# Raw first products of each later layer, its input in two VectorE operations and one ScalarE operation a tile, and the third output gate's product ahead of the first head

## The chip, the cores and the metric

The kernel runs on one core of one Trainium2 chip. The metric is the device time of one execution in microseconds; below it is the median of three runs. Smaller is better.

## The reference

A first block (gated feed-forward, attention with a state-space mixer, a second feed-forward, a gated embedding) is followed by two layers of the same form, each of which joins a gated linear recurrence and a matrix memory with heads. Sequence length is 512, model width 1024, all in float32. What the change touches is the end of the first block and the beginning of each later layer, cut to this:

```python
gate = jax.nn.sigmoid(rmsnorm(h, norm_ple[i]) @ w_ple_gate[i])
h = h + gate * (p[i] @ w_ple[i])
x = rmsnorm(h, norm_final)                      # end of the first block
for l in range(DEPTH_2):                        # the two later layers
    mod = c_act @ w_ada[l] + b_ada[l]
    shift, scale, gate = jnp.split(mod, 3, axis=-1)
    h = rms_norm(x, norm_g[l]) * (1.0 + scale[:, None, :]) + shift[:, None, :]
    u = h @ w_in[l]                             # 1024 x 5120
    rg_x, rg_z, ml_x, ml_o, ml_z = jnp.split(u, split_pts, axis=-1)
    y_rg = rglru(conv(rg_x), ...) * jax.nn.silu(rg_z)
    y_ml = mlstm_branch(ml_x, ml_o, ...) * jax.nn.silu(ml_z)
    y = jnp.concatenate([y_rg, y_ml], axis=-1) @ w_out[l]
    x = x + gate[:, None, :] * y
```

A norm is a factor for each position; so `h @ w_in` is the factor times the product of the unnormalised x (with the gain in it), plus `shift @ w_in`, which is the same for all positions.

## The kernel before

Activations lie transposed: model width in 8 tiles of 128 partitions, 512 positions along the free axis. A weight block is 128x128. Each float32 product is made of three matmuls in the engine's rounded float32 form (`mm3`, lines 125 to 127): high weight by high input, high weight by low input, low weight by high input. So each input tile is split in two (`xnh`, `xnl`), and so are the weights: the stream brings them in chunks of 8 blocks (512 KB), ScalarE makes the high half of a chunk (`whi`, line 96) and VectorE the low half (`wlo`, line 98). A chunk is split when the fifth block of the chunk two before it is fetched (`Stream.get`), unless `hold` is set; the split stands in the queues of both engines at that place of the program.

Each engine works through its own list in order. A norm is made in steps: ScalarE squares each tile (`nsq`, `nacc`, line 149), VectorE and GpSimd add them up, TensorE sums over the partitions by matmuls with ones (line 165, `early` for the first seven tiles, `mean` for the last), VectorE takes the root in ten short operations (`ncol`), TensorE transposes it to a row (line 195), and ScalarE copies the row (`nrow`, line 198).

The stages that matter here, in order:

- `ffn2`, the second feed-forward. A list of small pieces of work for the later layers (`second_prepare`: the products of `w_ada`, and the load and split of `p`) is dealt out between its products.
- `ple`, the gate stage: for each of 8 output tiles m a product of 8 blocks, a second product of 2 blocks for tile m-1, and then on VectorE the multiplication with the row (line 1282), on ScalarE tanh (1283), and on VectorE two operations that give the new `h[m]` (1287, 1288). `on_tile` squares it for two norms: the closing norm of the first block, and that of the first layer (`between` combines both).
- the first seam (`between`) and the second (`renorm`, ahead of layer 1): norm, then `modulate`, which makes the 8 input tiles from h, row, gain and shift: multiply by the row (`mt`, alternately on VectorE and GpSimd, line 1330), the affine on VectorE (`mx`, 1338) and with the high half on ScalarE (1337), and the low half on VectorE (1341).
- `layer`: first four products, `w_in` tiles 16 to 19, side by side (`proj4`), with VectorE's convolutions behind them (`ml_in`); then the order that `LAYER` writes out by hand. P*m* is the product of tile m, U*m* its use; 0 to 7 feed the recurrence, 24 to 27 are the output gates. `qkv` are the products of the first head pairs, `rg` the recurrence's gates, `hn` a head. `aside`, a list that `pump` works off twice a product, holds the residual's own norm and its store in layer 0.
- `out`: eight products of 16 blocks; each adds to the residual that is read back from memory (`xr`).

The order around the change, before: `P24 U24 P25 U25 P20 qkv0 ...` and further on `rg0 rq0 vr0 P26 U26 hn0 rs0 ...`.

Of the kernel before, what the change touches and what calls it, by code (L numbers as in the profile page):

```python
# [31 lines left out]
T = 512  # L32
DM = 1024
# [5 lines left out]
R1, R2 = 0.27, 0.26  # L39
# [8 lines left out]
GAPS = {"base": 288, "ffn1": 320, "ffn2": 0, "lay": 320, "mix2": 224, "ple": 256}  # L48
# [81 lines left out]
class Norm:  # L130
# [3 lines left out]
    def __init__(self, k, n, pool=None, tail=False):  # L134
        self.k, self.n, self.i = k, n, 0
        self.tail, self.head = tail, None
        self.pool = pool or k.work
        self.acc = []

    def add(self, src, scale=1.0):  # L140


        k, i = self.k, self.i
        own = i < 2 or (self.tail and i == self.n - 1)
        if own:
            sq = self.pool.tile([128, T], F32, name="nacc", bufs=3 if self.pool is k.work else 6)
# [3 lines left out]
        if own:  # L150
            self.acc.append(sq)
        elif i % 2:
            k.nc.gpsimd.tensor_add(self.acc[1], self.acc[1], sq)  # L153
        else:
            k.nc.vector.tensor_add(self.acc[0], self.acc[0], sq)
        self.i += 1
        if self.i == self.n - self.tail:
            eng = k.nc.vector if self.tail else k.nc.gpsimd
            eng.tensor_add(self.acc[0], self.acc[0], self.acc[1])
# [1016 lines left out]
def second_prepare(k, pool, ins):  # L1176
# [15 lines left out]
    for l in range(2):  # L1192
# [83 lines left out]
def ple(k, pool, xs, norm, pt, on_tile, early):  # L1276
# [3 lines left out]
    def gate1(m, pg):  # L1280
        ts[m] = pool.tile([128, T], F32, name="pleg", bufs=2)
# [16 lines left out]
    for m in range(8):  # L1298
# [12 lines left out]
        k.ws.hold = m == 7  # L1311
# [4 lines left out]
    early()  # L1316


def modulate(k, l, norm, gg, scr):
# [3 lines left out]
    xs, ts = [], []  # L1323
    with k.tc.tile_pool(name=f"modulate{l}", bufs=3) as tmp:
        def scale(d):
            t = tmp.tile([128, T], F32, name="mt", bufs=4)
            if d % 2:
                nc.gpsimd.tensor_mul(t, k.h[d], norm.row)
            else:
                v.tensor_mul(t, k.h[d], norm.wide)  # L1330
            ts.append(t)
        for d in range(3):
            scale(d)
        for d in range(8):
            x = tmp.tile([128, T], F32, name="mx")
            hi, lo = xtile(k, "xnh"), xtile(k, "xnl")
            nc.scalar.activation(hi, ts[d], AF.Identity, scale=gg[:, d:d + 1], bias=L.mod[:, d:d + 1])
            v.tensor_scalar(x, ts[d], gg[:, d:d + 1], L.mod[:, d:d + 1], op0=OP.mult, op1=OP.add)
            if d + 3 < 8:
                scale(d + 3)  # L1340
            v.tensor_sub(lo, x, hi.bitcast(F32))
            xs.append((hi, lo))
            if d == 1:
                k.ws.release()
            k.dbg(f"hh{l}{d}", x)
    return xs


def between(k, scr, nf, ng):

    nc, v = k.nc, k.nc.vector
    gg = k.work.tile([128, 8], F32, name="gg")
    gf = k.vec[:, VEC["norm_final"][0]:VEC["norm_final"][0] + 8]
    v.tensor_mul(gg, gf, k.lay[0].gs)
    nf.part1(root=False)
    ng.mean()
    ms = k.work.tile([128, 4], F32, name="nmt", bufs=2)
    v.scalar_tensor_tensor(ms, nf.ms, 1e-6, ng.ms, op0=OP.mult, op1=OP.add)  # L1360
    ng.col = k.work.tile([128, 4], F32, name="ncol", bufs=2)
    rsqrt(k, ng.col, ms)
    ng.part2()
    xs = modulate(k, 0, ng, gg, scr)
    rsqrt(k, nf.col, nf.ms)

    def root():
        nf.part2()

    def residual(d):  # L1370
        v.scalar_tensor_tensor(k.h[d], k.h[d], gf[:, d:d + 1], nf.row, op0=OP.mult, op1=OP.mult)
        nc.sync.dma_start(scr["x"][d], k.h[d])
        k.dbg(f"x2{d}", k.h[d])
    return xs, [root] + [lambda d=d: residual(d) for d in range(8)]


def renorm(k, l, norm, scr):
    norm.part1()
    norm.part2()
    xs = modulate(k, l, norm, k.lay[l].gs, scr)  # L1380
    return xs, [lambda d=d: k.nc.sync.dma_start(scr["x"][d], k.h[d]) for d in range(8)]


LAYER = """P24 U24 P25 U25 P20 qkv0 D P21 U20 U21 mi2 vw P22 U22 P23 U23 qkv1 D mi3 vw P0 U0 qkv2 vw D qkv3 g0 vw g1 P1 U1 ri0 P8 g2 D P9 U8 g3 hw0 hs0 U9 rg0 rq0 vr0 P26 U26 hn0 rs0 rs1 rz0 rz1 vr1 P27 U27 hw1 f0 P2 U2 hs1 D P3 U3 ri1 u F0 P32 U32 P33 U33 D rg1 rq1 hn1 rs2 P10 U10 P11 f1 rs3 U11 P29 U29 rz2 hw2 P28 rz3 vr2 U28 P4 U4 hs2 P5 U5 ri2 u P34 rg2 rq2 F1 U34 P35 U35 hn2 rs4 P12 D P13 f2 D U13 U12 rs5 P31 rz4 vr3 hw3 P30 rz5 U30 U31 P6 U6 P7 U7 ri3 D u hs3 D P36 F2 rg3 U36 P37 rq3 hn3 rs6 P14 U37 rs7 u P15 f3 U14 U15 rz6 P38 D F3 rz7 U38 D P39 U39 vw"""
# [82 lines left out]
def layer(k, l, xs, aside, ins, scr, norm, out):  # L1467
# [4 lines left out]
    with ExitStack() as st:  # L1472
        pool = st.enter_context(k.tc.tile_pool(name=f"lay{l}", bufs=1))
        room(pool, "lay")
# [51 lines left out]
        G = k.ps.tile([128, T], F32, name="pm", bufs=2)  # L1526
# [393 lines left out]
        def x_read(m):  # L1920
            if m < 8:
                xr[m] = xtile(k, "xr", F32)
                nc.sync.dma_start(xr[m], scr["x"][m])
        k.phase = f"out{l}"
        for m in range(8):
            x_read(m)
        for m in range(8):
            if l and m == 7:
# [10 lines left out]
            norm.add(k.h[m])  # L1939
VEC = {}  # L1940
# [20 lines left out]
def body(tc, ins, out, dbg):  # L1961
    nc = tc.nc
    with ExitStack() as ctx:
# [16 lines left out]
               "y": dp.tile([512, 512], F32, name="scr_y"), "x": dp.tile([8, 128, T], F32, name="scr_x"),  # L1980
# [70 lines left out]
        k.const2 = pool("const2")  # L2051
        k.onehot = k.const2.tile([8, 4, 128], F32R, name="onehot")
# [4 lines left out]
        with tc.tile_pool(name="prep2", bufs=1) as pp:  # L2057
# [4 lines left out]
            pt = []  # L2062
            ple_p = tc.tile_pool(name="ple", bufs=1)
            with ple_p as lp:
                room(lp, "ple")
                def load_p():
                    for d in range(2):
                        t = lp.tile([128, T], F32, name=f"p{d}")
                        nc.sync.dma_start(t, ins["pT"][d * 128:(d + 1) * 128])
                        pt.append(t)  # L2070

                def split_p():
                    for d in range(2):
                        pt[d] = split_plain(k, lp, pt[d], f"pp{d}", 1)
                k.fill.steps += [(0.1, load_p), (0.1, lambda: None), (1.2, split_p)]
                swiglu(k, st["xs"], st["norm"], "ffn2_w1", "ffn2_w3", "ffn2_w2", (6, 6, 5, 5),
                       lambda d: feed("norm_ple", d), R2, ((0, 1, 5), (1, 0, 7)), "ffn2")
                k.fill.drain()
                k.phase = "ple"
                with tc.tile_pool(name="sums", bufs=1) as np_:  # L2080
                    nf, ng = Norm(k, 8, np_, True), Norm(k, 8, np_, True)

                    def done(m):
                        nf.add(k.h[m])
                        ng.add(k.h[m], k.v("norm_final", m))
                    ple(k, lp, st["xs"], st["norm"], pt, done, lambda: (nf.early(), ng.early(0.0)))
                    xs, aside = between(k, scr, nf, ng)
        norm = None
        for l in range(2):
            norm = Norm(k, 8, tail=True)  # L2090
            k.phase = f"layer{l}"
            layer(k, l, xs, aside, ins, scr, norm, out)
# [132 lines left out]
```

## Time and profile before

| | |
|---|---|
| time, median of 3 runs | 1997.68 us (1996.73 to 1998.62) |
| the profiled execution | 1996.86 us, its span 1995.1 us |
| TensorE matmul busy | 1931.2 us, 97% |
| VectorE busy | 1311.4 us, 66% |
| ScalarE busy | 821.4 us, 41% |
| GpSimd busy | 164.4 us, 8% |
| mean granted TensorE clock | 0.982 of full speed |

The profile is of one execution. A busy time counts the instructions of an engine, not what waits; a row of a timeline gives the start of a group of like instructions in us from the start of the span, its length, and in brackets the idle time ahead of it with the engine that ended it. The time of the stages can be read from the names: the gate stage is 1061 to 1118 us, the first seam begins there, and the second at 1554.

### The profile page before, as it was taken

How to read it: one execution, taken by the hardware profiler on the slowest of the kernel's cores; microseconds unless marked ns; L12 is line 12 of the kernel's file. 1: busy time of each engine (PE TensorE's matmuls, PEld its weight loads, DVE VectorE, ACT ScalarE, POOL GpSimd, SP SyncE). 2: the span in 40 equal slices, each digit the busy share in tenths (PEclk: the TensorE clock that was granted, in tenths of full speed). 3: DMA queues.
4: the chain of work that ended last, by engine and by line, in shares of the span. 5: the costliest groups of instructions: out<-in, count | busy, mean ns of one | idle time of the engine just before them, and what ended most of it. 6: DMA issues, size and time to landing. Idle time of an engine off the chain costs nothing. (4 is left out here: it accounts for less than half of the span.)

```text
span 1995.1 us, 24709 instructions
## 1 busy us (share of the span) xinstructions
PE 1931.2 (97%) x9320; PEld 1581.3 (79%) x9320; DVE 1311.4 (66%) x2157; ACT 821.4 (41%) x1233; POOL 164.4 (8%) x225
## 2 busy tenths in 40 slices
PE   8999999998999999999999799999999899999997
PEld 6888888887867888888878687888888677887886
DVE  7766576678655575665666675887763666877843
ACT  5323232436555432232244445555432354555521
POOL 1000000111233100000001100101000100101001
PEclk9999999998899999999999899999999899999999
DMA  5335445465301365455433143222242243222241
GB/s 184 103 116 154 158 139 159 143 194 171 103 1 33 117 218 180 158 197 190 162 104 92 55 147 118 74 75 86 88 153 87 64 156 109 70 89 86 74 155 56
DMA packets 101400, 240.10 MB, mean 120 GB/s; under 512 B 24472, under 2 KB 37528, under 8 KB 101280
## 3 DMA queue, kind: packets, MB, share of 16 engines
q1 hardware_dynamic: 100592, 237.82, 37.6%
q8 instruction: 73, 1.20, 0.2%
q10 hardware_dynamic: 688, 0.70, 0.1%
q14 instruction: 47, 0.39, 0.1%
HBM read 216.19 MB, written 21.10 MB: 119 GB/s over the span
## 5 line engine op out<-in xcount | busy, mean ns | idle before, releaser
L98 DVE TENSOR_TENSOR wlo<-wstage,whi 128x1024 fp32r<-128x1024 f32 (+1 forms) x305 | 377.3, 1245 | 147.6 <-ACT whi L96 143.8
L96 ACT ACTIVATE whi<-wstage 128x1024 fp32r<-128x1024 f32 (+1 forms) x306 | 314.0, 1045 | 139.9 <-PE pasecond L126 43.1
L276 ACT ACTIVATE t<-t 128x512 f32<-128x512 f32 x44 | 27.9, 634 | 158.5 <-DVE t L275 158.5
L127 PE MATMUL pahead<-xnh,wlo 128*128 128x512 f32 x208 | 81.3, 391 | 3.4 <-DVE wlo L98 3.4
L125 PE MATMUL pahead<-xnh,whi 128*128 128x512 f32 x208 | 83.3, 400 | 0.0
L153 POOL TENSOR_TENSOR nacc<-nacc,nsq 128x512 f32<-128x512 f32 x20 | 26.8, 1343 | 680.9 <-ACT nsq L149 680.9
L126 PE MATMUL pahead<-xnl,whi 128*128 128x512 f32 x208 | 81.1, 390 | 0.0
L125 PE MATMUL pbfirst<-xnh,whi 128*128 128x512 f32 x176 | 70.4, 400 | 7.6 <-ACT whi L96 6.5
L125 PE MATMUL pbhead<-xnh,whi 128*128 128x512 f32 x192 | 76.9, 400 | 0.0
L1509 DVE SCALAR_TENSOR_TENSOR conv<-cpad,vec,conv 128x512 f32<-128x512 f32 x96 | 72.2, 752 | 5.6
L127 PE MATMUL pbhead<-xnh,wlo 128*128 128x512 f32 x192 | 75.5, 393 | 0.0
L126 PE MATMUL pbhead<-xnl,whi 128*128 128x512 f32 x192 | 75.3, 392 | 0.0
L126 PE MATMUL pbfirst<-xnl,whi 128*128 128x512 f32 x176 | 69.5, 395 | 0.3 <-DVE xnl L222 0.3
L127 PE MATMUL pbfirst<-xnh,wlo 128*128 128x512 f32 x176 | 69.2, 393 | 0.0
L125 PE MATMUL pbsecond<-xnh,whi 128*128 128x512 f32 x176 | 68.9, 392 | 0.0
L125 PE MATMUL pafirst<-xnh,whi 128*128 128x512 f32 x176 | 68.7, 390 | 0.0
L127 PE MATMUL pafirst<-xnh,wlo 128*128 128x512 f32 x176 | 68.6, 390 | 0.0
L127 PE MATMUL pbsecond<-xnh,wlo 128*128 128x512 f32 x176 | 68.5, 389 | 0.0
L126 PE MATMUL pbsecond<-xnl,whi 128*128 128x512 f32 x176 | 68.5, 389 | 0.0
L126 PE MATMUL pafirst<-xnl,whi 128*128 128x512 f32 x176 | 68.5, 389 | 0.0
L127 PE MATMUL pasecond<-xnh,wlo 128*128 128x512 f32 x176 | 68.5, 389 | 0.0
L125 PE MATMUL pasecond<-xnh,whi 128*128 128x512 f32 x176 | 68.5, 389 | 0.0
(762 smaller groups left out, 5229.9 us busy)
## 6 DMA issues: line engine op xcount, KB each, us to landing
wstage<-in_wpack_dram SPq DMA_DIRECT2D x304, 512.0 KB, 3.7
adaw<-in_wada_dram SPq DMA_DIRECT2D x48, 512.0 KB, 4.5
scr_v<-vv SPq DMA_DIRECT2D x16, 256.0 KB, 2.2
vr<-scr_v SPq DMA_DIRECT2D x16, 256.0 KB, 4.4
xr<-scr_x SPq DMA_DIRECT2D x16, 256.0 KB, 5.8
h<-in_xT_dram SPq DMA_DIRECT2D x8, 256.0 KB, 5.8
s5vw<-scr_wq SPq DMA_DIRECT2D x64, 32.0 KB, 2.0
s5vb<-in_s5bq_dram SPq DMA_DIRECT2D x8, 256.0 KB, 2.7
```

What stands on the lines that cost most here:

```text
L96: k.nc.scalar.activation(hi[:, s], st[:, s], AF.Copy)
L98: eng.tensor_sub(lo[:, s], st[:, s], hi[:, s].bitcast(F32))
L125: mm(ps, w[0], x[0], start=start, stop=False)
L126: mm(ps, w[0], x[1], start=False, stop=False)
L127: mm(ps, w[1], x[0], start=False, stop=stop)
L153: k.nc.gpsimd.tensor_add(self.acc[1], self.acc[1], sq)
L276: nc.scalar.activation(t1, t1, AF.Silu)
L1509: v.scalar_tensor_tensor(c, xp[:, 1 + j:1 + j + T], w(j), c, op0=OP.mult, op1=OP.add)
```

## The change

1. In the gate stage each new `h[m]` is split at once, times the gain but without the row, in a high half on ScalarE and a low half on VectorE (`split_raw`), and stored to memory as the residual. Tile 6 is split ahead of its squares, whose sums wait for tile 7. In layer 0's `out` the same is done for layer 1.
2. The layer's first four products run on these raw tiles in the order `RAW`. At given numbers of blocks, hooks run the steps of the norm (early sums, mean, row: 8, 10, 14 in layer 0 and 1, 3, 9 in layer 1) and then one input tile every second block. A finished raw product is multiplied with the row on VectorE, and `sw`, the product of shift and `w_in`, is added on ScalarE (`raw_pad`).
3. `modulate` makes a tile in two operations on VectorE and one on ScalarE between them; GpSimd has none.
4. `sw` is made in `ffn2`'s list: per layer two groups of four transposes, four loads of 512 KB and four reductions on VectorE.
5. `p` is loaded and split at the start of the gate stage, not in `ffn2`'s list.
6. The closing norm's factor is put on the residual in layer 0's `out` (one operation a tile), not in `aside`.
7. `P26 U26` stand behind `P25 U25`, not ahead of `hn0`. `hold` is no longer set at the end of `ple` and of `out`.

The pool of the layers is shared and opened before the gate stage. The diff, cut to its core:

```diff
-R1, R2 = 0.27, 0.26
+R1, R2 = 0.27, 0.30
-GAPS = {"base": 288, "ffn1": 320, "ffn2": 0, "lay": 320, "mix2": 224, "ple": 256}
+GAPS = {"base": 288, "ffn1": 320, "ffn2": 160, "lay": 384, "mix2": 224, "ple": 256}
...
+        def shift(n, L=L, box=box):
...
+            for j in range(4):
+                nc.tensor.transpose(ps[:, j * 128:(j + 1) * 128],
+                                    L.mod[:, 4 * n + j:4 * n + j + 1].to_broadcast([128, 128]), k.ident)
+            nc.scalar.activation(box["sh"][:, n * T:n * T + T], ps, AF.Copy)
...
+            v.tensor_tensor_reduce(out=junk, in0=boxes["s", i], in1=box["sh"], scale=1.0, scalar=0.0,
+                                   op0=OP.mult, op1=OP.add, accum_out=L.sw[:, i:i + 1])
...
+def split_raw(k, src, g, hi, lo):
+    k.nc.scalar.activation(hi, src, AF.Copy, scale=g)
+    k.nc.vector.scalar_tensor_tensor(lo, src, g, hi.bitcast(F32), op0=OP.mult, op1=OP.subtract)
+    return hi, lo
...
+    def tile(d):
+        t = k.ytile("mt")
+        g, b = gg[:, d:d + 1], L.mod[:, d:d + 1]
+        v.scalar_tensor_tensor(t, k.h[d], g, norm.wide if d == 0 else norm.row, op0=OP.mult, op1=OP.mult)
+        hi, lo = xtile(k, "xnh"), xtile(k, "xnl")
+        nc.scalar.activation(hi, t, AF.Identity, bias=b)
+        v.scalar_tensor_tensor(lo, t, b, hi.bitcast(F32), op0=OP.add, op1=OP.subtract)
+        xs.append((hi, lo))
...
+RAW = [(m, d) for m in range(4) for d in range(7)]
+RAW = RAW[:14] + [(0, 7)] + RAW[14:21] + [(1, 7)] + RAW[21:] + [(2, 7), (3, 7)]
+def seam(k, l, norm, gg, early, mean, at):
+    xs, tile = modulate(k, l, norm, gg)
+    hooks = dict(zip(at, (early, mean, norm.part2)))
+    for d in range(8):
+        hooks[at[2] + 1 + 2 * d] = lambda d=d: tile(d)
+    return xs, hooks
...
+    return (*seam(k, 0, ng, gg, early, mean, (8, 10, 14)), [lambda: rsqrt(k, k.closing, nf.ms)])
...
+    return (*seam(k, l, norm, k.lay[l].gs, norm.early, norm.part1, (1, 3, 9)), [])
...
-LAYER = """P24 U24 P25 U25 P20 qkv0 D P21 ... U9 rg0 rq0 vr0 P26 U26 hn0 rs0 ...
+LAYER = """P24 U24 P25 U25 P26 U26 P20 qkv0 D P21 ... U9 rg0 rq0 vr0 hn0 rs0 ...
...
+        def raw_pad(i, ps):
+            xp = pool.tile([128, T + 4], F32, name="cpad", bufs=5)
+            nc.gpsimd.memset(xp[:, 0:4], 0.0)
+            v.tensor_mul(xp[:, 4:], ps, before.row)
+            nc.scalar.activation(xp[:, 4:], xp[:, 4:], AF.Identity, bias=L.sw[:, i:i + 1])
...
+        for n, (i, d) in enumerate(RAW):
+            mm3(k, banks[i], k.ws.get((win, d, 16 + i)), raw[d], d == 0, d == 7)
+            if n in hooks:
+                hooks[n]()
+            if d == 7:
+                raw_pad(i, banks[i])
...
+            if l == 0:
+                v.scalar_tensor_tensor(xr[m], xr[m], k.v("norm_final", m), pb, op0=OP.mult, op1=OP.mult)
...
+                raw.append(split_raw(k, k.h[m], k.lay[1].gs[:, m:m + 1], xtile(k, "xnh"), tile("xnl", F32R)))
+                nc.sync.dma_start(scr["x"][1, m], k.h[m])
```

What stands in the lists of the engines at three places. First VectorE in the middle of the gate stage, from one `h` to the next (`pleg` is the gate's tile, `pbple` and `paple` banks of TensorE's products, `nacc` a sum of squares). Before:

```order
L1288 SCALAR_TENSOR_TENSOR h<-pleg,h 128x512 [waits DVE_49]
L155 TENSOR_TENSOR nacc<-nacc,nsq 128x512 [waits Activation_49] x2
L1282 TENSOR_TENSOR pleg<-pbple,nrow 128x512 [waits PE_49]
L98 TENSOR_TENSOR wlo<-wstage,whi 128x1024 [waits DMAHW1_49,Activation_49]
L1287 SCALAR_TENSOR_TENSOR pleg<-pleg,paple 128x512 [waits PE_49]
L1288 SCALAR_TENSOR_TENSOR h<-pleg,h 128x512 [waits DVE_49]
```

With the change, at the same place:

```order
L1325 SCALAR_TENSOR_TENSOR h<-pleg,h 128x512 [waits DVE_49]
L159 TENSOR_TENSOR nacc<-nacc,nsq 128x512 [waits Activation_49] x2
L1357 SCALAR_TENSOR_TENSOR xnl<-h,gg,xnh 128x512 [waits DVE_49,Activation_49]
L1319 TENSOR_TENSOR pleg<-pbple,nrow 128x512 [waits PE_49]
L98 TENSOR_TENSOR wlo<-wstage,whi 128x1024 [waits DMAHW5_49,Activation_49]
L1324 SCALAR_TENSOR_TENSOR pleg<-pleg,paple 128x512 [waits PE_49]
L1325 SCALAR_TENSOR_TENSOR h<-pleg,h 128x512 [waits DVE_49]
```

The low half of the raw tile has come in ahead of the next gate's multiplication, and it waits for ScalarE.

Second, VectorE in the first seam from the norm's root on (`ncol`). Before:

```order
L213 SCALAR_TENSOR_TENSOR ncol<-rsa,rsy 128x4 [waits DVE_49]
L1330 TENSOR_TENSOR mt<-h,pm 128x512 [waits Activation_49]
L1330 TENSOR_TENSOR mt<-h,pm 128x512
L1338 TENSOR_SCALAR mx<-mt,gg,mod_5923 128x512 [waits DVE_49]
L1341 TENSOR_TENSOR xnl<-mx,xnh 128x512 [waits DVE_49,Activation_49]
L1338 TENSOR_SCALAR mx<-mt,gg,mod_5923 128x512 [waits Pool_49]
L1330 TENSOR_TENSOR mt<-h,pm 128x512
L1341 TENSOR_TENSOR xnl<-mx,xnh 128x512 [waits DVE_49,Activation_49]
```

With the change:

```order
L220 SCALAR_TENSOR_TENSOR ncol<-rsa,rsy 128x4 [waits DVE_49]
L98 TENSOR_TENSOR wlo<-wstage,whi 128x1024 [waits DMAHW4_49,Activation_49]
L1529 TENSOR_TENSOR cpad<-pagates_9195,nrow 128x512 [waits Activation_49]
L1370 SCALAR_TENSOR_TENSOR mt<-h,gg,pm 128x512 [waits PE_49]
L1373 SCALAR_TENSOR_TENSOR xnl<-mt,mod_5924,xnh 128x512 [waits Activation_49]
L1370 SCALAR_TENSOR_TENSOR mt<-h,gg,nrow 128x512
L1373 SCALAR_TENSOR_TENSOR xnl<-mt,mod_5924,xnh 128x512 [waits Activation_49]
L1370 SCALAR_TENSOR_TENSOR mt<-h,gg,nrow 128x512
```

A tile has two rows where it had two or three; a tile's first operation stands behind the low half of the tile before, where `mt` ran up to three tiles ahead. The finished raw product (`cpad`) stands in the same list.

Third, TensorE ahead of the first head of layer 0 (`pc` takes the recurrence's gates, `pbgates` P26, `pahead` the head). Before, the end of P26 and the head:

```order
L125 MATMUL pbgates0_10363<-xnh_9212,whi_10258 128x512
L126 MATMUL pbgates0_10363<-xnl_9213,whi_10258 128x512
L127 MATMUL pbgates0_10363<-xnh_9212,wlo_10259 128x512
L1758 MATMUL pahead00_10400<-Wd_10284,vr_10359 128x128
L1758 MATMUL pahead00_10400<-Wo_10285,vr_10359 128x128
```

With the change:

```order
L125 MATMUL pc_10421<-rxh_10321,whi_10284 128x512
L126 MATMUL pc_10421<-rxl_10323,whi_10284 128x512
L127 MATMUL pc_10421<-rxh_10321,wlo_10285 128x512
L1793 MATMUL pahead00_10453<-Wd_10370,vr_10445 128x128
L1793 MATMUL pahead00_10453<-Wo_10371,vr_10445 128x128
```

The 24 matmuls of P26 have gone from between the recurrence's gates and the head; they now stand ahead of P20, behind the seam.

## Rows read from the trace of the kernel before

**Rows 1.** The page, part 1: busy us, share of the span, instructions.

```profile
PE 1931.2 (97%) x9320; PEld 1581.3 (79%) x9320; DVE 1311.4 (66%) x2157; ACT 821.4 (41%) x1233; POOL 164.4 (8%) x225
```

**Rows 2.** Table by stretches: from:to, us, busy by engine, granted clock, DMA.

```profile
1118.00:1161.00 43.00, 32.04 (x135) 25.85 (x134) 29.51 (x60) 16.41 (x22) 5.33 (x9) 0.80 0.23 73
1550.00:1590.00 40.00, 32.62 (x134) 26.01 (x134) 24.18 (x41) 14.52 (x19) 5.32 (x9) 0.83 0.21 67
```

**Rows 3.** Timeline of TensorE, first seam: start us, us, instruction, [idle before <-releaser].

```profile
1118.17 0.39 PE L127 MATMUL pbple<-pp1h,wlo 128*128 128x512 f32 x1
...
1125.02 3.57 PE L165 MATMUL pm<-ones,nacc 128*128 128x1 f32 x16 [2.26 <-ACT nacc L149]
...
1161.06 0.60 PE L195 MATMUL pm<-ident,ncol 128*128 128x128 f32 x4
...
1178.77 0.40 PE L125 MATMUL pbgates<-xch,whi 128*128 128x512 f32 x1
```

**Rows 4.** Timeline of VectorE, gate stage.

```profile
1077.83 0.69 DVE L1288 SCALAR_TENSOR_TENSOR h<-pleg,h 128x512 f32<-128x512 f32 x1
...
1109.56 1.23 DVE L98 TENSOR_TENSOR wlo<-wstage,whi 128x1024 fp32r<-128x1024 f32 x1 [1.65 <-ACT whi L96]
...
1111.42 0.69 DVE L1288 SCALAR_TENSOR_TENSOR h<-pleg,h 128x512 f32<-128x512 f32 x1
...
1117.24 0.69 DVE L1288 SCALAR_TENSOR_TENSOR h<-pleg,h 128x512 f32<-128x512 f32 x1
...
1123.61 0.69 DVE L1288 SCALAR_TENSOR_TENSOR h<-pleg,h 128x512 f32<-128x512 f32 x1
```

**Rows 5.** Timeline of ScalarE, gate stage.

```profile
1112.20 0.63 ACT L149 ACTIVATE nsq<-h 128x512 f32<-128x512 f32 x1 [2.67 <-DVE h L1288]
1112.74 0.71 ACT L149 ACTIVATE nsq<-h,vec 128x512 f32<-128x512 f32 x1
...
1113.88 1.05 ACT L96 ACTIVATE whi<-wstage 128x1024 fp32r<-128x1024 f32 x1
```

**Rows 6.** Timeline of VectorE at the end of the second feed-forward.

```profile
1060.19 0.68 DVE L305 SCALAR_TENSOR_TENSOR h<-pasecond,h 128x512 f32<-128x512 f32 x1
1061.67 0.75 DVE L222 SCALAR_TENSOR_TENSOR xnl<-h,vec,xnh 128x512 fp32r<-128x512 f32 x1 [0.80 <-ACT xnh L221]
1062.33 0.69 DVE L155 TENSOR_TENSOR nacc<-nacc,nsq 128x512 f32<-128x512 f32 x1
```

**Rows 7.** Timeline of VectorE, first seam.

```profile
1132.86 1.29 DVE L1330 TENSOR_TENSOR mt<-h,pm 128x512 f32<-128x512 f32 x2 [1.90 <-ACT nrow L198]
...
1159.85 0.55 DVE L1507 TENSOR_SCALAR conv<-cpad,vec 128x512 f32<-128x512 f32 x1 [1.99 <-ACT cpad L1501]
...
1177.52 0.68 DVE L1546 TENSOR_TENSOR xcl<-xcs,xch 128x512 fp32r<-128x512 f32 x1
```

**Rows 8.** Timeline of TensorE, second seam.

```profile
1554.36 0.39 PE L127 MATMUL pbout<-ymh,wlo 128*128 128x512 f32 x1
1556.26 1.05 PE L165 MATMUL pm<-ones,nacc 128*128 128x1 f32 x8 [1.51 <-ACT nacc L149]
...
1589.51 0.39 PE L125 MATMUL pagates<-xnh,whi 128*128 128x512 f32 x1
```

**Rows 9.** Timeline of ScalarE, second seam.

```profile
1560.74 0.60 ACT L198 ACTIVATE nrow<-pm 128x512 f32<-128x512 f32 x1 [4.54 <-PE pm L195]
```

**Rows 10.** Timeline of TensorE, first head of layer 0.

```profile
1269.43 0.39 PE L125 MATMUL pbgates<-xnh,whi 128*128 128x512 f32 x1
...
1274.88 0.38 PE L1758 MATMUL pahead<-Wd,vr 128*128 128x128 f32 x2
...
1292.01 0.39 PE L127 MATMUL pbhead<-xnh,wlo 128*128 128x512 f32 x1
```

**Rows 11.** TensorE's waits in the second feed-forward: us in total, times, longest.

```profile
PE pasecond L125 <- ACT gh L233: 2.3, 1, 2.3
```

**Rows 12.** Timeline of VectorE, first head of layer 0.

```profile
1290.27 1.23 DVE L98 TENSOR_TENSOR wlo<-wstage,whi 128x1024 fp32r<-128x1024 f32 x1 [1.65 <-ACT whi L96]
```

More of the change, by code (lines that the diff above doesn't have):

```diff
@@ L145, in add @@
         if own:
-            sq = self.pool.tile([128, T], F32, name="nacc", bufs=3 if self.pool is k.work else 6)
+            sq = self.new("nacc")
         else:
@@ L1273, in second_prepare, with ple @@
     return steps
-def ple(k, pool, xs, norm, pt, on_tile, early):
+def ple(k, xs, norm, pt, on_tile):
     nc, v = k.nc, k.nc.vector
@@ L1315, in ple, with modulate @@
     gate2(7, pps[7])
-    early()
-def modulate(k, l, norm, gg, scr):
+def split_raw(k, src, g, hi, lo):
+    k.nc.scalar.activation(hi, src, AF.Copy, scale=g)
+    k.nc.vector.scalar_tensor_tensor(lo, src, g, hi.bitcast(F32), op0=OP.mult, op1=OP.subtract)
+    return hi, lo
+def modulate(k, l, norm, gg):
     nc, v = k.nc, k.nc.vector
     L = k.lay[l]
[L1323 to L1346, printed above, removed]
@@ L1349, in between @@
[L1349 to L1374, printed above, removed]
@@ L1377, in renorm @@
[L1377 to L1384, printed above, removed]
+    xs = []
@@ new lines, with between, early, mean @@
+RAW = RAW[:14] + [(0, 7)] + RAW[14:21] + [(1, 7)] + RAW[21:] + [(2, 7), (3, 7)]
[5 more added lines that the diff above has]
+    return xs, hooks
+def between(k, nf, ng, gg):
+    v = k.nc.vector
+    def early():
+        nf.early()
+        ng.early(0.0)
+    def mean():
+        nf.mean()
+        ng.mean()
+        ms = k.work.tile([128, 4], F32, name="nmt", bufs=2)
+        v.scalar_tensor_tensor(ms, nf.ms, 1e-6, ng.ms, op0=OP.mult, op1=OP.add)
+        ng.col = k.work.tile([128, 4], F32, name="ncol", bufs=2)
+        rsqrt(k, ng.col, ms)
+    return (*seam(k, 0, ng, gg, early, mean, (8, 10, 14)), [lambda: rsqrt(k, k.closing, nf.ms)])
@@ L1464, in ending, with layer @@
     last(1, 6, False, nc.sync)
-def layer(k, l, xs, aside, ins, scr, norm, out):
+def layer(k, l, raw, xs, hooks, aside, before, ins, scr, norm, out):
     nc, v = k.nc, k.nc.vector
@@ L2061, in body @@
             k.fill.steps += second_prepare(k, pp, ins)
[L2062 to L2087, printed above, removed]
@@ new lines, in body @@
+        for d in range(2):
+            hi, lo = k.ytile(f"pp{d}h", F32R), k.ytile(f"pp{d}l", F32R)
+            nc.scalar.activation(hi, pt[d], AF.Copy)
+            nc.vector.tensor_sub(lo, pt[d], hi.bitcast(F32))
+            pt[d] = hi, lo
+        nf, ng = Norm(k, 8, k.ytile, True), Norm(k, 8, k.ytile, True)
+        gg = k.work.tile([128, 8], F32, name="gg")
+        gf = k.vec[:, VEC["norm_final"][0]:VEC["norm_final"][0] + 8]
+        nc.vector.tensor_mul(gg, gf, k.lay[0].gs)
+        raw = []
@@ new lines, in body, with done @@
+        later = []
+        def done(m):
+            if m == 6:
+                raw.append(split_raw(k, k.h[m], gg[:, m:m + 1], k.ytile("xnh", F32R), k.ytile("xnl", F32R)))
+            nf.add(k.h[m], 1.0, later if m == 6 else None)
+            ng.add(k.h[m], k.v("norm_final", m), later if m == 6 else None)
+            for f in later if m == 7 else ():
+                f()
+            if m != 6:
+                raw.append(split_raw(k, k.h[m], gg[:, m:m + 1], k.ytile("xnh", F32R), k.ytile("xnl", F32R)))
+            nc.sync.dma_start(scr["x"][0, m], k.h[m])
@@ L2089, in body @@
+        ple(k, st["xs"], st["norm"], pt, done)
+        before = ng
+        xs, hooks, aside = between(k, nf, ng, gg)
         for l in range(2):
@@ L2091, in body @@
             k.phase = f"layer{l}"
-            layer(k, l, xs, aside, ins, scr, norm, out)
+            raw = layer(k, l, raw, xs, hooks, aside, before, ins, scr, norm, out)
             if l == 0:
-                xs, aside = renorm(k, 1, norm, scr)
+                before = norm
+                xs, hooks, aside = renorm(k, 1, norm)
         return k.ws
```

105 lines of the change are left out of this document (71 added, 34 removed).

## The prediction

> **What bounds the kernel now.** First the page's busy shares [rows 1]: TensorE 1931.2 us of a span of 1995.1, VectorE 1311.4. The reader is to see that only some 64 us of TensorE's time are idle at all. Then the table by stretches [rows 2]: between the stages TensorE is busy 32.04 of 43 us at a mean clock of 0.80, and 32.62 of 40 us at 0.83. These are the two seams, where the input of a layer is made. The work in each is four products of eight blocks, three matmuls a block. 24 matmuls of P26 take 5.45 us [rows 10], 0.227 apiece, 0.68 a block, so the 96 cost 21.8 us at 2.4 GHz. Seam 0 runs from the last matmul before it to the transposes behind it, 1118.17 to 1161.06 [rows 3], and loses 21.1; seam 1 from 1554.36 to 1589.51 [rows 8] loses 13.3.
>
> Then TensorE's own timeline [rows 3]: the last matmul at 1118.17, the last sums of squares not before 1125.02. Last, VectorE behind the seam [rows 7]: input tiles from 1132.86, convolutions from 1159.85, and the low half of the second convolved tile from 1177.52 to 1178.20. TensorE asks for it at 1178.77 [rows 3], in qkv0. The slack is 0.6 us: behind seam 0 VectorE, not TensorE, is the one to follow.
>
> **The change, part by part.** *ffn2.* The wait of 2.3 us for the gate tile [rows 11] came from splitting p in ScalarE's line; p goes to the next stage, and the wait with it. 16 transposes come: four in 0.60 us with overlap, about 0.4 net (the group at 1161.06) [rows 3], 1.6 in all. Eight reductions more lie on VectorE beside TensorE's products. Sum -0.7, bounds -2.3 and +1.
>
> *The gate stage.* Before, VectorE's step from h to h is 5.82 us in the last (1111.42 to 1117.24) [rows 4]; ScalarE's two squares and the tanh lie beside it. Now the raw split stands between h and the next gate: 0.78 us from the start of h to the first square (1111.42 to 1112.20), 0.54 to the second, 1.14 for that one and the tanh [rows 5], 1.08 for the weights' high half on ScalarE, and 1.86 from VectorE's low half of them to the next h (1109.56 to 1111.42) make 5.4. New in the line are the tile's high half on ScalarE and its low half on VectorE, 0.80 and 0.69 at their nearest rows [rows 6], and the gate's product, which no longer lies beside the squares, 0.7 with its handover: 7.5 us a step. TensorE needs ten blocks, 6.8 us, a step. From h0 at 1077.83, six steps of 7.5 and 1.6 for the step with two weight splits put h6 at 1124.5, against 1117.24: 7.3 late. TensorE can run ahead only by its banks and stops a few microseconds in this stage; the end of the seam is not set there but by h7.
>
> *Seam 0.* h7, 6.5 behind h6, starts near 1131, against 1123.61. Four additions of squares of 0.65 follow, so the early column sums that stand behind the ninth raw block start near 1134 and TensorE waits some 4 us in front of them. Two sums of 1.0, two blocks, two sums put the mean at 1138.7. From its column sums to the end of the row seam 1 took 4.0 us (1556.26 with 1.05, then 1560.74 with 0.60) [rows 8, 9], which gives a row at 1142.7, where before it stood at 1132.8. So the row is 9.9 later. Then comes VectorE's list: four rescaled raw sums (0.6 each), two weight splits of 1.15 and eight tiles stand ahead of the first convolution, which waits 0.8 more for ScalarE to add the bias to the last sum. A tile is a product, ScalarE's high half, and a low half that waits for it, strictly in turn. The same pattern in the stage before takes 2.14 us (1060.19 to 1062.33) [rows 6], so eight take 17.1. 2.4 + 2.3 + 17.1 + 0.8 = 22.6: convolutions from 1165.3, 5.5 later than before. From there to the end of that low half there were 18.3 us [rows 7], to be followed by a weight split of 1.15 that P20 needs, and the last six blocks of P20 (4.1 us) and the four gate matmuls (0.9): qkv0 starts at 1189.4, 10.6 later. P26, 5.45 us [rows 10], is done by then. Net +5.2, with P24, P26 and P20 each waiting 4 to 6 us.
>
> The Trainium skill, "VectorE: DVE Perf Modes", section "Rules for kernel authors", says to keep the number of VectorE operations small and not to care about the semaphores between them. By it a tile would fall from two and a half operations to two and cost its own time only. The trace disagrees for this order: VectorE idled 0.80 us in front of the low half, waiting for ScalarE [rows 6]. What the rule would give is the first rival's time below.
>
> *Seam 1.* Here the row comes 3.0 later: hooks at blocks 2 and 4 wait for the last tile's square as before, and the raw block, the sums and the transposes share TensorE. VectorE's list is 1.4 longer by one weight split. The convolutions start at 1564.3 + 24.0 = 1588.3, about where they stood, and qkv0 at 1612.3. Before, it came some 17.4 behind the seam, as 1161.06 and 1178.77 show for seam 0, at 1606.9. Less P26's 5.45 that is nothing; I take -0.3 for the transposes that no longer stand alone. Before, the idle time of this seam was short, so there is little to win.
>
> *P26 at the first head.* Before, it ran from 1269.43 to 1274.88 between the recurrent gates and hn0 [rows 10]. The gates' follow-up on VectorE and ScalarE ends in the weight split of 1290.27 to 1291.50 [rows 12], which P2 takes at 1292.01 [rows 10], 0.5 us of slack. Its start is set by the gates, ahead of P26, so without P26 TensorE arrives 5.45 earlier and waits up to 4.9 a layer. The lower bound is nothing, if the follow-up moves too. I take the middle, 2.45, twice: +4.9.
>
> *At no cost.* The residual's eight products leave layer 0 for out0, where VectorE follows products of 10.9 us a tile; the store of the residual goes out during the gate stage. If these were uncovered, 8 x 0.69 = 5.5 us would be lost. p is loaded ahead of the gate stage, whose first projection comes nearly two products later.
>
> Sum: -0.7 + 5.2 - 0.3 + 4.9 = +9.1. The profiled run took 1996.86, so 2006.0. The median of the three runs is 0.8 above that run; I don't add it.
>
> **Rivals.** *VectorE keeps up (faster).* If the alternation costs only VectorE's own time, a tile is 1.22 us, not 2.14, and eight save 7.4 a seam; if the raw split hides beside the gate loop, h7 comes 7.6 earlier. Then -0.7 + (5.2 - 7.4 - 7.6) + (-0.3 - 7.4) = -18.2, 1979, with nothing lost at the first head; with half of both gains and half of that loss it is about 1993. The middle, 1985, is this rival's time. For it speaks the size of the idle time, 21.1 and 13.3 us, against at most 64 in the whole. Against it speak the 0.80 us of waiting in [rows 6] and VectorE's 0.6 us of slack in [rows 3, 7]. It decides when the row of seam 0 comes before 1136.
>
> *The clock falls in the new waits (slower still).* After the idle time of seam 0 the sixteen column sums at 1125.02 took 3.57 us, where eight took 1.05 in seam 1 [rows 3, 8]: the lower of the two levels, 1.2 GHz instead of 2.4. The waits of 4 to 6 us at the early sums, at P24's last tile, at P26 and at P20 might each bring that. A mean of 0.80 over 43 us [rows 2] is 17 us at the lower level, idle time with it. If half of that, 8 us, comes once more behind each seam, it loses 2 x 4: 2014. Against it: the waits that set the end are VectorE's, and a slow TensorE may hide beside them. The Trainium skill, "TensorE: Matmul & The Clock Gate", section "HAM oscillation — how this bites in real kernels", tells of this: bursts of products with waits between them start each burst slow. By it the time would be this rival's; the row at 1125.02 agrees with it.
>
> *It cancels (no change).* The raw products do their work, VectorE's backlog behind seam 0 costs half (2.6) and the first head nothing: -0.7 + 2.6 - 0.3 = +1.6, 1998.5.
>
> **How the numbers follow.** Forecast 0.40, VectorE keeps up 0.36, clock 0.12, cancels 0.12. A difference under 0.2%, 4 us, can't be told from none. So faster 0.36, the same 0.12, slower 0.52. The forecast's own range is 2001 to 2011: 4.9 for the first head up or down. Cases of both signs hold most of the chance, so the range reaches into the rival on the fast side, 1984, leaving 0.12 below, and up to 2013, leaving 0.08 above.
>
> **What would show it.** In the profile after: h6 of the gate stage at 1124 rather than 1117; the row of seam 0 near 1142 and the first convolution near 1165; a step of 2.14 us from tile to tile on VectorE, with a wait of 0.8 for ScalarE in each; waits of TensorE for the low weight halves in P26 and P20, and in P2 behind the first head; no wait in ffn2. I am wrong if the tiles follow each other in 1.3 us, if h6 stays near 1118, or if TensorE does not wait between seam 0 and qkv0.

## The result: 22 us slower

The changed kernel took 2020.39 us (median of 4 runs, 2018.35 to 2022.09), the kernel before beside it 1998.15 (1996.73 to 2001.39): ratio 1.011, 95% interval 1.0094 to 1.0126. The forecast had the side right and the size wrong: +9.1 in its sum, 2006, range to 2013.

The page of the changed kernel, part 1, answers to [rows 1]: a span of 2017.5 us against 1995.1, with 13.8 us more of TensorE's busy time for 16 matmuls more.

```profile
PE 1945.0 (96%) x9336; PEld 1584.6 (79%) x9336; DVE 1330.2 (66%) x2189; ACT 831.7 (41%) x1252; POOL 156.7 (8%) x217
```

The reader is to see that most of the loss is counted as busy: the matmuls that were there before took longer. Marks on TensorE's timeline in the two profiles give the steps (first matmul of the gate stage, of the first head, of the output products, of layer 1's first head, of layer 1's output products):

| stretch | forecast | measured |
|---|---|---|
| ffn2, to the gate stage (1061.33, now 1058.97) | -0.7 | -2.4 |
| gate stage and seam 0, to the first head (1274.88, now 1283.03) | +5.2 | +10.5 |
| heads of layer 0, to its output products (1466.59, now 1480.55) | +2.45 | +5.8 |
| seam 1, to layer 1's first head (1703.07, now 1719.10) | -0.3 | +2.1 |
| heads of layer 1, to the output products (1893.57, now 1915.98) | +2.45 | +6.4 |
| sum | +9.1 | +22.4 |

The second row holds what the first had won as well: at the first head the changed kernel is 8.2 us late, where the sum had 4.5.

TensorE's waits from the gate stage to qkv0, changed kernel (us in total, times, longest):

```profile
PE pbgates L127 <- DVE wlo L98: 4.1, 1, 4.1
PE pm L172 <- DVE nacc L162: 4.0, 1, 4.0
PE pbple L125 <- DVE pleg L1319: 2.4, 3, 1.7
...
PE pagates L127 <- DVE wlo L98: 1.2, 1, 1.2
```

From the top these are P20 at a weight split behind the convolutions, the early sums behind the ninth raw block, the stops in the gate stage, and P26 at an earlier weight split. All four were forecast, and 4 to 6 us each for P24, P26 and P20; only P20's 4.1 is of that size (P26 1.2, the last tiles of P24 2.2 in all). VectorE in the gate stage, where [rows 4] had a last step of 5.82 us:

```profile
1108.34 0.69 DVE L1325 SCALAR_TENSOR_TENSOR h<-pleg,h 128x512 f32<-128x512 f32 x1
...
1115.87 0.69 DVE L1325 SCALAR_TENSOR_TENSOR h<-pleg,h 128x512 f32<-128x512 f32 x1
1118.55 0.75 DVE L1357 SCALAR_TENSOR_TENSOR xnl<-h,gg,xnh 128x512 fp32r<-128x512 f32 x1 [1.99 <-ACT xnh L1356]
1119.21 0.69 DVE L1319 TENSOR_TENSOR pleg<-pbple,nrow 128x512 f32<-128x512 f32 x1
...
1123.41 0.69 DVE L1325 SCALAR_TENSOR_TENSOR h<-pleg,h 128x512 f32<-128x512 f32 x1
```

These steps take 7.53 and 7.54 us; 1.99 of the second is VectorE's wait for the raw high half, which ScalarE makes behind the two squares. h6 starts at 1123.41, not 1117.24. The 5.82 of before was a short step: from h0 to h6 the mean is 6.57 in [rows 4], and now 7.88 (h0 at 1076.14). And the first seam, where [rows 7] had its first convolution at 1159.85:

```profile
1144.56 0.74 DVE L1370 SCALAR_TENSOR_TENSOR mt<-h,gg,pm 128x512 f32<-128x512 f32 x1
1146.09 0.75 DVE L1373 SCALAR_TENSOR_TENSOR xnl<-mt,mod,xnh 128x512 fp32r<-128x512 f32 x1 [0.79 <-ACT xnh L1372]
1146.76 0.74 DVE L1370 SCALAR_TENSOR_TENSOR mt<-h,gg,nrow 128x512 f32<-128x512 f32 x1
...
1166.84 0.54 DVE L1543 TENSOR_SCALAR conv<-cpad,vec 128x512 f32<-128x512 f32 x1
```

A tile takes 2.20 us (2.14 forecast), 0.79 of it idle for ScalarE.

What was not in the sum is the clock. The changed kernel by short stretches (from:to, us, busy us of PE, PEld, DVE, ACT, POOL, then the granted clock, then DMA):

```profile
1131.00:1139.00 8.00, 7.02 (x31) 6.47 (x31) 4.06 (x8) 3.22 (x5) 0.00 (x0) 0.57 0.52 166
...
1162.00:1169.00 7.00, 6.65 (x14) 4.47 (x15) 5.88 (x9) 4.04 (x6) 0.00 (x0) 0.51 0.24 75
...
1186.00:1190.00 4.00, 3.78 (x10) 3.01 (x11) 3.58 (x8) 3.01 (x4) 0.00 (x0) 0.57 0.46 135
```

```profile
1619.00:1627.00 8.00, 5.69 (x15) 4.49 (x16) 6.60 (x8) 4.12 (x6) 0.10 (x1) 0.57 0.38 105
```

0.51 to 0.57 is all but wholly the lower level, 1.2 GHz, each time behind waits or in one (the 4.0 us from 1128 on, waits for tiles around 1160, the 4.1 from 1182 on, and in seam 1 a wait of 4.1 from 1617 on). The seam before had its slow time too, 0.80 in [rows 2], and from 1120 to 1195 us the mean is even the same in both kernels. The kernel before, then the changed one:

```profile
1120.00:1195.00 75.00, 65.49 (x298) 53.24 (x299) 56.69 (x98) 33.91 (x50) 6.01 (x13) 0.89 0.29 95
```

```profile
1120.00:1195.00 75.00, 63.16 (x250) 48.58 (x251) 54.90 (x94) 32.60 (x47) 1.29 (x10) 0.89 0.25 76
```

But before, TensorE was busy for only 9.9 of the 17.1 us that it had at the lower level there; now for 16.0 of 17.1. Work stands in it, and part of that work is in the chain that sets the end (changed kernel, timeline of TensorE: the column sums behind the first of these waits, P20's first matmul behind the last, and qkv0):

```profile
1131.98 3.54 PE L172 MATMUL pm<-ones,nacc 128*128 128x1 f32 x16 [4.02 <-DVE nacc L162]
...
1186.22 0.79 PE L127 MATMUL pbgates<-xnh,wlo 128*128 128x512 f32 x1 [4.09 <-DVE wlo L98]
...
1192.37 0.39 PE L125 MATMUL pagates<-xch,whi 128*128 128x512 f32 x1
```

### The profile page after: what moved, and what is told of

It is laid out like the page before. It is cut to its first block, busy times and chain, and to the rows that moved or that the text cites. A ratio compares the mean times of both kernels' runs of the same rounds, so it can differ in the third digit from the quotient of the medians.

```text
span 2017.5 us, 24788 instructions
## 1 busy us (share of the span) xinstructions
PE 1945.0 (96%) x9336; PEld 1584.6 (79%) x9336; DVE 1330.2 (66%) x2189; ACT 831.7 (41%) x1252; POOL 156.7 (8%) x217
```

## Experiments

The three suspected causes were undone one by one, then together, and the first was also put alone into the kernel before. The ratio behind each time is to the kernel before, run beside it; that one took 1997.7 to 1998.7 each time, so medians are set against each other here to about a microsecond.

**P26 back ahead of the first head** (in the changed kernel):

```diff
-LAYER = """P24 U24 P25 U25 P26 U26 P20 qkv0 ... rg0 rq0 vr0 hn0 ...
+LAYER = """P24 U24 P25 U25 P20 qkv0 ... rg0 rq0 vr0 P26 U26 hn0 ...
```

> The changed kernel, but P26 U26 stand again between the recurrent gates and hn0. Theory (in the changed kernel VectorE's list sets qkv0 and P26 runs in its shadow; what the heads lose is mostly granted clock, not the wait that P26 covered): qkv0 stays within 2 us of the changed kernel's 1192.4 although 5.45 us of work are gone ahead of it, the waits of 0.5 us behind hn0 go, and the time rises by 4 to 8 us, to about 2026. Rival (the cover of P26 is what the heads miss, and the falls of the clock there follow from it): the heads give back 5 us a layer, the time falls to about 2014.

2010.65 us (2007.99 to 2012.96; before 1998.72; 1.0058, 1.0036 to 1.0081), some 10 us less than the changed kernel. My theory fell, in the sign of the time and in qkv0, which now starts at 1179.73, 12.6 us earlier and not within 2; the rival stands. TensorE's waits from the seam into qkv0:

```profile
PE pm L172 <- DVE nacc L162: 4.0, 1, 4.0
PE pbgates L126 <- DVE xcl L1581: 3.6, 1, 3.6
...
PE pagates L127 <- DVE wlo L98: 1.2, 1, 1.2
```

With 5.45 us of work fewer in this stretch TensorE waits no longer than with it: 3.6 for the second convolved tile in qkv0, where it was 4.1 for the weights in P20. P26 in the seam had consumed blocks, and so brought forward the need for the weight split behind the convolutions: it bought itself a wait of its own. The two stretches of the heads, from the first head to the output products (columns as above):

```profile
1281.49:1473.52 192.03, 189.32 (x968) 158.80 (x967) 151.44 (x259) 98.23 (x136) 17.09 (x22) 0.99 0.27 81
1709.66:1904.75 195.09, 192.26 (x964) 161.01 (x963) 151.36 (x259) 98.34 (x136) 16.62 (x22) 0.97 0.26 79
```

Against the changed kernel's 197.52 and 196.88 the heads gave back 5.5 us in layer 0 and 1.8 in layer 1; the rest of what these two profiles differ by lies ahead of the heads, 1.5 and 2.4, though P26 now stands there, behind the gates.

**Squares and raw split deferred in the gate stage:**

```diff
-        on_tile(m)
...
             gate1(m, pgs[m])
+            on_tile(m - 1)
...
     gate2(7, pps[7])
+    on_tile(7)
```

> The changed kernel, but in the gate stage the squares and the raw split of tile m-1 are issued behind the gate's product and tanh of tile m. Theory (the split stood in the loop from h to h): a step of VectorE falls from 7.47 to about 6.6 us, h6 starts near 1118 instead of 1123.4, TensorE's waits in the stage (0.5, 1.7, 0.4, 0.4) go, and the time falls by 4 to 6 us, to about 2015. Rival (the end of the seam is set by VectorE's tiles and convolutions alone, and an earlier h6 is waited away): within 1.5 us of 2020.

2015.08 us (2011.79 to 2017.05; 1.0084, 1.006 to 1.0108): 5.3 less, as the theory said. VectorE's step:

```profile
1104.05 0.69 DVE L1325 SCALAR_TENSOR_TENSOR h<-pleg,h 128x512 f32<-128x512 f32 x1
...
1110.60 0.69 DVE L1325 SCALAR_TENSOR_TENSOR h<-pleg,h 128x512 f32<-128x512 f32 x1
```

Four of the six steps from h0 to h6 take 6.55 us, under TensorE's 6.8 (the other two 8.50 and 7.36); h6 starts at 1117.96, and TensorE's waits behind the gate's bank are gone.

**Each tile's first operation ahead of the low half of the tile before it:**

```diff
-        v.scalar_tensor_tensor(lo, t, b, hi.bitcast(F32), op0=OP.add, op1=OP.subtract)
+        todo.append(lambda: v.scalar_tensor_tensor(lo, t, b, hi.bitcast(F32), op0=OP.add, op1=OP.subtract))
+        if d:
+            todo.pop(0)()
+        if d == 7:
+            todo.pop(0)()
+    todo = []
```

> The changed kernel, but in both seams a tile's first operation is issued ahead of the low half of the tile before it. Theory (VectorE idles 0.79 us in each tile for ScalarE, and its list sets qkv0): a step from tile to tile falls from 2.20 to about 1.4 us, the convolutions start 6 us earlier in each seam, TensorE's waits for wlo at P26 and P20 (1.2 and 4.1, 3.3 and 4.1 us) shrink to under 2, and the time falls by 9 to 13 us, to about 2009. Rival (TensorE sets it: raw blocks and P24 to P20 fill the time anyway): 0 to 3 us faster, about 2018.

2010.13 us (2009.19 to 2014.78; 1.0061, 1.0038 to 1.0084): 10.3 less. VectorE in seam 0:

```profile
1147.90 0.75 DVE L1370 SCALAR_TENSOR_TENSOR mt<-h,gg,nrow 128x512 f32<-128x512 f32 x1
1148.56 0.75 DVE L1374 SCALAR_TENSOR_TENSOR xnl<-mt,mod,xnh 128x512 fp32r<-128x512 f32 x1
1149.22 0.75 DVE L1370 SCALAR_TENSOR_TENSOR mt<-h,gg,nrow 128x512 f32<-128x512 f32 x1
...
1162.25 0.54 DVE L1548 TENSOR_SCALAR conv<-cpad,vec 128x512 f32<-128x512 f32 x1
```

A tile in 1.32 us. Two parts of the expectation missed: in seam 0 the convolutions start 4.6 us earlier, not 6, and P20 still waits 4.1 and P26 2.4 for the weights, only earlier.

**Both seam edits:**

> Both edits: squares and raw split behind the next gate's product, and the tile's first operation ahead of the last low half. Theory: the gains add in the first seam, 14 to 18 us, about 2004; what stays against the kernel before is the heads' 6 us a layer less what the seams then gain. Rival (one of them covers the other, since VectorE's idle time and the lateness of h7 are waited for together): no more than the better of the two alone, about 2009.

2005.88 us (10 runs, 2002.37 to 2007.3; 1.0034, 1.0024 to 1.0044): 14.5 less than the changed kernel. 5.3 and 10.3 add up to 15.6, so the two gains nearly add.

**P26 alone, in the kernel before** (the same edit of the order, forwards: from right ahead of the first head into the seam):

> The kernel before with one thing of the change alone: P26 U26 behind P25 U25. Theory (the move is bad by itself: in the seam it brings forward the weight split that stands behind the convolutions on VectorE, and behind hn0 TensorE waits and its clock falls): 8 to 13 us slower than before, about 2009, of which 5 to 6 a layer lie between hn0 and the output products; lower clock in the profile within 30 us behind the first head of each layer. Rival (the move only costs in the raw seam, where VectorE is late): within 3 us of before.

2007.87 us (2006.24 to 2009.58; before 1997.92; 1.0055, 1.0035 to 1.0076). This one line is +10 us, and the seam has no part in it: in its profile the first head starts at 1275.22, before at 1274.88. The loss is in the heads. To size it against what one kernel's executions differ by, each of the two kernels has a second profile:

> The kernel before once more, for its clock. Theory (the falls of the clock between the heads come with P26's move): as in the first profile, one stretch of 3.4 us at half clock behind hn0 of layer 0 and at most one more among the eight heads. Rival (they fall by chance in any execution): three or more among the eight heads, as in the changed kernel.

> The changed kernel once more, for its clock. Theory: four or more stretches at half clock among the eight heads again, one of them behind the first head of each layer, and about 2020. Rival (chance): a number like that of the kernel before, two or fewer, and then about 2012.

They took 2000.27 and 2021.17 (one execution each). The two head stretches of each profile. The kernel before, and its second profile:

```profile
1274.88:1466.59 191.71, 188.96 (x964) 158.50 (x963) 151.10 (x259) 98.38 (x136) 17.11 (x22) 0.99 0.27 80
1703.07:1893.57 190.50, 187.62 (x964) 157.43 (x963) 150.96 (x259) 98.50 (x136) 16.62 (x22) 1.00 0.27 81
```

```profile
1274.07:1469.19 195.12, 192.28 (x964) 161.05 (x963) 151.38 (x259) 98.35 (x136) 16.66 (x22) 0.97 0.26 79
1705.07:1897.02 191.95, 189.10 (x964) 158.56 (x963) 151.14 (x259) 98.35 (x136) 16.64 (x22) 0.99 0.27 81
```

The changed kernel (its second profile has 197.53 and 196.93), and P26 alone:

```profile
1283.03:1480.55 197.52, 193.32 (x969) 161.13 (x967) 153.18 (x262) 102.30 (x141) 17.71 (x24) 0.97 0.26 79
1719.10:1915.98 196.88, 192.97 (x965) 160.97 (x963) 152.80 (x262) 102.30 (x141) 17.76 (x24) 0.97 0.26 78
```

```profile
1275.22:1472.10 196.88, 192.96 (x964) 161.09 (x963) 152.79 (x262) 102.30 (x141) 17.73 (x24) 0.97 0.26 78
1707.70:1903.00 195.30, 191.36 (x964) 159.62 (x963) 152.78 (x262) 102.30 (x141) 17.70 (x24) 0.98 0.26 79
```

The same matmuls (964 to 969 records): TensorE idles 3.9 to 4.2 us a layer with P26 moved, against 2.8 before, and is busy longer at a lower clock, by 0.7 to 5.4 us according to which profiles are set against each other. The idle part is two waits behind the first head (changed kernel, timeline of TensorE):

```profile
1301.73 0.50 PE L125 MATMUL pbhead<-xnh,whi 128*128 128x512 f32 x1 [0.48 <-ACT whi L96]
...
1302.99 0.50 PE L127 MATMUL pbhead<-xnh,wlo 128*128 128x512 f32 x1 [0.53 <-DVE wlo L98]
```

P26 alone has the same two waits, 0.50 and 0.53 us. They are short because the follow-up of the gates got shorter as well. The kernel before, VectorE and then TensorE; last P26 alone, VectorE:

```profile
1277.96 1.23 DVE L98 TENSOR_TENSOR wlo<-wstage,whi 128x1024 fp32r<-128x1024 f32 x1 [0.92 <-ACT whi L96]
```

```profile
1293.37 0.39 PE L127 MATMUL pbhead<-xnh,wlo 128*128 128x512 f32 x1
```

```profile
1293.90 1.23 DVE L98 TENSOR_TENSOR wlo<-wstage,whi 128x1024 fp32r<-128x1024 f32 x1 [1.65 <-ACT whi L96]
```

In the kernel before, the split that P2 needs starts 20.8 us behind the end of the gates' products (1269.43 to 1290.27), with the split of 1277.96 in between; with P26 alone moved 18.7 (1275.22 to 1293.90), and none stands in between.

The two second profiles settle a part for each side. In the kernel before, the heads had one stretch at the lower level in the first profile, 3.4 us, 12.9 behind the first head of layer 0. In the second they have three, and none of them behind a first head:

```profile
1333.49:1336.90 3.41, 3.41 (x10) 2.67 (x9) 3.34 (x7) 2.13 (x3) 0.00 (x0) 0.50 0.27 61
1394.93:1401.75 6.82, 6.82 (x20) 5.56 (x20) 5.18 (x22) 1.02 (x2) 0.00 (x0) 0.50 0.54 180
1825.01:1828.42 3.41, 3.41 (x9) 2.64 (x9) 2.82 (x18) 0.38 (x1) 0.00 (x0) 0.50 0.82 247
```

Three was the rival's sign: the clock falls there in the kernel before as well, in some executions, and its two profiles differ by 4.9 us in the heads with the same waits. So of the 12.2 us in the table about 2.4 are the first profile's luck. The changed kernel has five in both of its profiles, 20.5 us in sum, with one behind the first head of each layer, as the theory said. Over all runs the two sorts do not overlap. With P26 in the seam (six profiles: the changed kernel twice, the seam edits single and together, P26 alone) the heads take 392 to 394 us in sum, 17.1 to 20.5 of them at the lower level. With P26 ahead of the head (five profiles: the kernel before twice, P26 back, and the two runs at the end of this section) they take 382 to 387, with 3.4 to 13.6.

**P26 behind the first head** (in the kernel before):

```diff
-... rg0 rq0 vr0 P26 U26 hn0 ...
+... rg0 rq0 vr0 hn0 P26 U26 ...
```

> The kernel before, with P26 U26 right behind hn0 instead of right ahead of it. Theory (the heads miss P26 as work that lies beside the follow-up of the recurrent gates; on which side of the head it stands does not matter): no waits of 0.5 us ahead of P2's weights, and within 3 us of the kernel before. Rival (it is the dense product ahead of the head's small matmuls that keeps the clock up): lower clock behind hn0 in both layers without any wait, 3 to 7 us slower than before.

1995.53 us (10 runs, 1994.17 to 2000.06; before 1997.71; 0.9991, 0.998 to 1.0003): no change that can be told, as the theory said. The waits of 0.5 us are not there, and the clock is at the upper level throughout (P26 now lies inside the two stretches):

```profile
1268.96:1464.73 195.77, 192.99 (x989) 161.99 (x987) 153.19 (x263) 103.70 (x143) 17.20 (x24) 1.00 0.25 79
1695.83:1891.60 195.77, 193.00 (x989) 162.00 (x988) 152.70 (x263) 103.69 (x143) 17.51 (x24) 1.00 0.26 79
```

P26 need not stand ahead of the head's small matmuls; of the three places tried, the two between the recurrent gates and P2 are alike, and the one in the seam costs 10 us.

**All three edits:**

> The changed kernel with the split deferred in the gate stage, the tiles issued one ahead, and P26 back ahead of hn0. Theory (losses of the seams and of the heads are separate and add): the first run with both seam edits stood 0.2 us behind the kernel before at hn0, 3.6 ahead in the second seam, and lost 5.8 and 6.2 in the heads; with P26 back these 12 go: about 1995, 2 to 5 us faster than the kernel before. Rival (P26 in the seam gave cover that the seams then lack): the seams lose 5 each again, about 2005.

1993.30 us (10 runs, 1990.92 to 1995.62; before 1997.92; 0.9977, 0.9968 to 0.9986). Faster than both kernels. The three edits alone gave 9.7, 5.3 and 10.3 us, 25.3 in sum; together they give 27.1, more than the whole loss. TensorE's waits from the raw blocks into qkv0:

```profile
PE pm L172 <- DVE nacc L162: 3.6, 2, 3.3
PE pagates L127 <- DVE wlo L98: 2.4, 1, 2.4
PE pbgates L126 <- DVE xcl L1587: 2.1, 1, 2.1
```

**And the norm's steps at other raw blocks:**

```diff
+RAW0 = RAW[:21] + [(0, 7)] + RAW[21:] + [(1, 7), (2, 7), (3, 7)]
...
-    return (*seam(k, 0, ng, gg, early, mean, (8, 10, 14)), ...
+    return (*seam(k, 0, ng, gg, early, mean, (12, 13, 17)), ...
...
-    return (*seam(k, l, norm, k.lay[l].gs, norm.early, norm.part1, (1, 3, 9)), [])
+    return (*seam(k, l, norm, k.lay[l].gs, norm.early, norm.part1, (1, 3, 6)), [])
...
-        for n, (i, d) in enumerate(RAW):
+        for n, (i, d) in enumerate(RAW if l else RAW0):
```

> The run with all three edits, and the norm's steps at other raw blocks: in layer 0 early sums, mean and row at blocks 12, 13 and 17 (not 8, 10, 14), in layer 1 at 1, 3 and 6 (not 1, 3, 9); the first raw product of layer 0 ends later for it. Theory (TensorE stands still at the early sums for 3.3 us with raw blocks left to run, and the row comes late for the tiles): the wait at the early sums falls under 1 us, the row of layer 0 comes 5 us and that of layer 1 2 us earlier, and the time falls by 4 to 8 us against the run with all three edits (1993.3), to about 1987, 10 us faster than the kernel before. Rival (VectorE's list behind the row sets the rest and its other work only closes up): within 2 us of 1993.

1991.07 us (5 runs, 1989.36 to 1993.18; before 1997.71; 0.9966, 0.9953 to 0.9978), 6.6 us faster than the kernel before. The waits in the same stretch:

```profile
PE pagates L126 <- DVE xnl L1375: 3.9, 2, 3.6
PE pbgates L126 <- DVE xcl L1588: 3.5, 1, 3.5
PE pm L172 <- DVE nacc L162: 0.9, 2, 0.5
```

The wait at the early sums fell from 3.6 to 0.9 as expected, and the row of layer 0 came 4.4 us earlier, but most of it came back in front of a tile's low half and of the convolved tile, and the convolutions started only 2.2 earlier. Against the run before it the median is 2.2 less, not 4 to 8, and the intervals of the two overlap, so that this gain is not clear of noise. The waits fit the rival, that VectorE's list sets the rest.

## Why the prediction was wrong

- *VectorE's list in gate stage and seam 0* was right in mechanism and nearly in size: h6 1123.4 for 1124.5, a tile 2.20 for 2.14, convolutions from 1166.8 for 1165.3, qkv0 at 1192.4 for 1189.4, P26 and P20 waiting for their weights. Undoing the two parts of it gave 5.3 and 10.3 us.
- *The step that failed* is "P26 at the first head". Alone the move is +10 us, against 4.9 in the sum, and both of its parts came out otherwise. The waits are 1.0 us a layer, not 2.45. [rows 10, 12] were misread: P2 takes that split with its seventh block, at 1293.37 and not at 1292.01, so the slack was 1.9 us and not 0.5; and the follow-up got 2.2 shorter, which the forecast had only as its lower bound. 5.45 less 1.9 and 2.2 is 1.4. The rest of the 10 us, some 4 a layer, goes with the granted clock: the heads of that run have 17.1 us at the lower level, where the two profiles of the kernel before have 3.4 and 13.6. At half the clock the difference can cost up to 6.8 us against the first and 1.7 against the second, so the clock's share is not settled to the microsecond. The forecast put the clock at nothing here; I looked for it in the seams alone.
- *P26 counted as gain in the seam* (5.45 "done by then") was no gain: with it back ahead of the head, the first head still came 1.5 us earlier in layer 0, and the stretch up to it was 2.4 shorter in layer 1.
- *The clock as a rival instead of a term.* With chance 0.12 it stood beside the forecast; it happened on top of it. From the early sums to the end of the mean the changed kernel took 8.0 us, where the sum's terms give 5.4: it had two column sums of 1.0, although [rows 3] show sixteen such matmuls at 3.57 behind a wait, and now they took 3.54. From the end of P20's wait to qkv0 it took 6.2 for 5.0, and in seam 1, by the same terms, 7.0 for 5.0, which can account for most of that seam's +2.1 where -0.3 was forecast. This is read from the rows; no run took the clock away by itself. My argument against it, that slow work hides beside VectorE's waits, holds only where the wait comes behind the work, as for the stretch at 1162: P26 and P20 wait for VectorE after it. The column sums and the end of P20 stand in the chain themselves.
- *ffn2* gave 2.4 for 0.7: the wait is gone, and the 16 transposes, all done by 943 us, cost at most 0.4 (at 1025 us, ahead of that wait, the changed kernel is 0.4 behind).
- *VectorE keeps up*, the fast rival, was not this kernel. The run with all three edits took 1993, the number of the rival's half-way case, but that is luck: its own sign, a row of seam 0 before 1136, did not come there (1142.4), P26 stands elsewhere, and the half-way terms add up to 1992.3.
- *Slips in the sums*, none over a microsecond: 1134 with two sums, two blocks and two sums is 1139.4, not 1138.7; 1165.3 with 18.3, 1.15, 4.1 and 0.9 is 1189.8, not 1189.4; the parts of the step make 7.6, not 7.5; 1161.06 to 1178.77 is 17.7, not 17.4.

What stays open: why the clock falls more often in the heads once P26 is gone. The runs show that it goes with P26's absence between the gates and P2 and not with the side of the head on which P26 stands. In every profile that has any, with the move or without, the falls begin at the same places: 12 to 14, 59 to 64 and 120 to 125 us behind a layer's first head; the move changes how many of them come. The two waits of half a microsecond lie 18 to 20 us behind it, so they do not set off the first of these falls, and the second profile of the kernel before has the other two without such waits. What does was not separated.

## What to carry to other kernels

A product that stands beside a long chain of VectorE and ScalarE work can be cover, also when the place it is to go to looks free: before moving it, ask what will be beside that chain afterwards; here either side of the head did, as long as it lay within the chain's length. Where two engines hand a tile to and fro, issue the next tile's first operation ahead of the second of the tile before: it took 10 us off here for a handful of lines. And where TensorE gets new waits of some microseconds with work behind them, price that work by a row that stands behind such a wait, in the sum and not beside it.

## What the runs showed of the hardware

One kernel's executions can differ by the clock with the same waits: in the two profiles of the kernel before, the head stretches take 382.2 and 387.1 us, with 3.4 and 13.6 us at the lower level of the granted clock. A single pair of profiles can so be off by 5 us of 2000; timed medians and a second profile are needed before a difference of that size in one stretch is read.
